# A four-layer hybrid network on one core: the first 400 tokens taken in two parts, with two engines in written order

## The chip, the core and the metric

The kernel runs as one program on one core of a Trainium2 chip. The metric is device time in microseconds (us). Engines are named as in the profile: PE is TensorE (matmuls; PEld are its weight loads), DVE is VectorE, ACT is ScalarE, POOL is GpSimd, SP is SyncE, which here only starts DMA transfers. Each engine works through its own queue in order and waits there for semaphores of the others.

## The reference

`x` (1024 tokens of 1024 features) is put behind 16 learned "meta" tokens, so there are 1040 tokens. Four layers follow, each `h = h + branch(rmsnorm(h))`: attention with a window of 128 tokens, an mLSTM, an HGRN2, and attention again. Only the start of the first attention layer matters here:

```python
def rmsnorm(x, g):
    xf = x.astype(jnp.float32)
    y = xf * lax.rsqrt(jnp.mean(xf * xf, axis=-1, keepdims=True) + EPS)
    return (y * g.astype(jnp.float32)).astype(x.dtype)

def attention_branch(u, w_in, q_gain, k_gain, sinks, w_out, valid, pos):
    q, k, v, z = _split(u @ w_in, (A_W, A_KVW, A_KVW, A_W))
    q = rope(rmsnorm(q.reshape(bsz, lp, A_HEADS, A_HD), q_gain), pos)
    k = rope(rmsnorm(k.reshape(bsz, lp, A_KV, A_HD), k_gain), pos)
    ...
    return (o * jax.nn.silu(z.astype(jnp.float32))).astype(u.dtype) @ w_out
```

`u = rmsnorm(h)` needs, for each token, a sum over all 1024 features before anything can be multiplied with weights.

## The kernel before

**Layout.** Features lie on the 128 partitions in 8 blocks (`KT`, index `k`), tokens along the columns: `x` is a tile of 128 x 8 x 1040. Tokens are worked through in three chunks (`CHUNKS`): columns 0 to 400, 400 to 784, 784 to 1040; below they are chunk 0, 1 and 2.

**Numbers in two halves.** Products run in the type F32R, whose operands are rounded. So each operand is split into a high and a low part (`split`: ACT casts the value to the high part, line 187; DVE subtracts it from the value for the low part, line 188), and a product is three matmuls: high x high, high x low, low x high. The normalised input `u` becomes the tiles `uh` and `ul`; a weight tile becomes `wh` and `wl`, made from a raw tile `wr` in two halves of 512 columns. Raw tiles have 2 buffers (`RAWS`), loaded by SP.

**The norm of a chunk.** For each of the 8 feature blocks ACT squares `x` (`sq`, line 369) and DVE sums the squares (line 373); PE multiplies the sum by a tile of ones in plain f32 to sum over partitions (`stat`, line 381; below: a ones product); ACT makes the reciprocal root by Ln and Exp (lines 353 and 354). `PARTS` is the number of pieces in which this is done per chunk. Then `unit`, for each block: DVE multiplies `x` by gain and reciprocal root (line 407, below: a multiply), and `split` gives `uh` and `ul`. For the 16 meta tokens POOL copies both parts into a small tile `um` (line 412).

**Products.** `proj` makes K and Q (line 254): 8 blocks x 3 matmuls per chunk, with the tokens as the moving side. `proj_v` makes V by blocks of tokens (lines 295 and 299): block 0 is the 16 meta tokens, taken from `um`, blocks 1 to 3 the rest of chunk 0. V's weights come in two tiles (blocks k 0 to 3, and 4 to 7); each token block is so two groups of matmuls, written `vg[0][2 * block + half]`.

**Order.** The PE queue is written out by hand as a list of steps (`steps`); on DVE, ACT and POOL a scheduler places instructions. A step may have a `pre` (a weight load and its split), which is issued up to `LOOKAHEAD` ns ahead. For the first layer the head list is `kv`: two K steps, V's groups of the first half, the other K steps, V's second half. `FIRST` says at which share of the head's cost the norms of chunks 1 and 2 are inserted.

**Names in the change.** `row()` is one of 9 buffers of 128 x 1040; it holds rope tables, K and attention rows. `psa()` and `psj()` take one of 8 PSUM banks. `tc.manual_schedule(engines=...)` makes the named engines keep the order in which the code issues.

Of the kernel before, what the change touches and what calls it, by code (L numbers as in the profile page):

```python
# [9 lines left out]
F32 = mybir.dt.float32  # L10
# [5 lines left out]
P = 128  # L16
# [9 lines left out]
LAST_CHUNKS = [(16, 384), (400, 384), (784, 256)]  # L26
CHUNK_BLOCKS = [(0, 1, 2, 3), (4, 5, 6), (7, 8)]
# [17 lines left out]
PARTS = 2, 2, 2  # L45
FIRST = 0.3, 0.9, 0.3, 0.7
# [62 lines left out]
def hybrid_kernel(ctx: ExitStack, tc: tile.TileContext, ins, out, layers=(0, 1, 2, 3)):  # L109
# [57 lines left out]
    g.memset(um.bitcast(F32), 0.0)  # L167

    def load_x(n):
        c0, cn = CHUNKS[n]  # L170
        for k in range(KT):
            sp.dma_start(x[:, k, c0 : c0 + cn], ins["xT"][k, :, c0 : c0 + cn])

    load_x(0)
    sp.dma_start(ident, ins["ident"])
    sp.dma_start(ngain, ins["ngain"])

# [46 lines left out]
    def weights(src, kind, inrow=False):  # L224
# [5 lines left out]
        for z in (slice(0, 512), slice(512, 1024)):  # L230
            raw = wpool.tile([P, 512], F32, tag="raw", name=nm("wr"), bufs=RAWS)
# [5 lines left out]
    def proj(src, evac, chunks=CHUNKS):  # L237
        st = {}

        def pre():  # L240
            st["w"] = weights(src, "m")

        groups = []
        for n, (c0, cn) in enumerate(chunks):
            grp = []
            for part in range(4):
                def fn(n=n, c0=c0, cn=cn, part=part):
                    if part == 0:
                        st[n] = psj()
                    h, l = st["w"]  # L250
                    acc = st[n]
                    for k in (2 * part, 2 * part + 1):
                        for i, (a, b) in enumerate(((h, uh), (h, ul), (l, uh))):
                            pe.matmul(acc[:, :cn], a[:, k, :], b[:, k, c0 : c0 + cn],  # L254
                                      start=(k == 0 and i == 0), stop=(k == KT - 1 and i == 2))
                    if part == 3:
                        evac(acc, n, c0, cn)

                grp.append([6 * cn * MM, fn, pre if (n == 0 and part == 0) else None])
            groups.append(grp)  # L260
        return groups
# [9 lines left out]
    def proj_v(src0, src1, evac):  # L271
        st = {}

        def pre0():
            st[0] = weights(src0, "v")

        def pre1():
            st[1] = weights(src1, "v")
# [84 lines left out]
    class Norm:  # L363
# [11 lines left out]
        def stat(self, n, part=0, parts=1):  # L375
            cn = CHUNKS[n][1]

            def fn():
                if part == 0:
                    self.ps[n] = psa()  # L380
                pe.matmul(self.ps[n][:, :cn], ones, self.acc[n], start=(part == 0), stop=(part == parts - 1))
                if part == parts - 1:
                    rstd_from(self.ps[n], self.acc[n], cn, D)

            return [4 * cn * MM, fn, None]

        def stats(self, n, parts):

            c0, cn = CHUNKS[n]
# [11 lines left out]
        def unit(self, n, k):  # L401
# [12 lines left out]
            return [0.0, fn, None]  # L414

# [24 lines left out]
    def layer_a(i, j, first, last, fin):  # L440
# [4 lines left out]
        def enter():  # L445
            R["mix"] = mix = new_mix()
            R["masks"] = masks = mix.tile([P, A_MASKS], F32, name=nm("masks"))
            sp.dma_start(masks, ins["a_masks"])
            R["cons"] = cons = mix.tile([P, 34], F32, name=nm("cons"))
            sp.dma_start(cons, ins["a_cols"][j])  # L450
            v.tensor_scalar(cons[:, 0:1], cons[:, 0:1], 0.125, None, op0=ALU.mult)
# [62 lines left out]
        def qk_proj(src, gcol, work, fsplit, ch, scales=None):  # L514
# [45 lines left out]
            return proj(src, evac, ch), [finish(n, *c) for n, c in enumerate(ch)]  # L560
# [152 lines left out]
        kg0, kfin0 = qk_proj(win[0], 1, work_rows(3), k_split(0), CHUNKS)  # L713
        kg1, kfin1 = qk_proj(win[1], 1, work_rows(1), k_split(1), CHUNKS)
        vg = proj_v(win[2], win[3], v_evac)
# [16 lines left out]
        head[0].insert(0, [0.0, enter, None])  # L732
# [596 lines left out]
    steps += norm.stats(0, PARTS[0]) + [norm.unit(0, k) for k in range(KT)]  # L1329
    tail = None  # L1330
    for pos, i in enumerate(layers):
# [10 lines left out]
        if i % 3 == 0:  # L1342
            head, body, oa, ob = layer_a(i, i // 3, tail is None, i == 3, fin)
# [30 lines left out]
    while steps[k][2] is None:  # L1374
        k += 1
    steps[k][2]()
    steps[k][2] = None
    load_x(1)
    k = 0
    for n, (cost, fn, pre) in enumerate(steps):  # L1380
# [5 lines left out]
        if n == 0:  # L1386
            load_x(2)
# [118 lines left out]
```

## Time and profile before

| | |
|---|---|
| median of 3 runs (lowest, highest) | 2607.71 us (2605.75, 2611.24) |
| the profiled execution | 2610.83 us, its span 2609.0 us |
| busy in the span | PE 2558.0 us (98%), DVE 1980.3 (76%), ACT 1725.9 (66%), POOL 154.1 (6%) |
| first product of chunk 0 / of chunk 1 starts | 14.90 us / 36.95 us |
| mean granted PE clock | 0.995 |

Times in rows of the profile are us from the span's start. A row of the timeline gives the start, the length, the engine, the line, the operation, what it writes and reads by the program's names (buffer numbers left out), the shape, a count, and in brackets how long the engine stood idle before it and what ended that. A group row has the count, busy us, the mean in ns, and the idle time before. Neighbouring matmuls overlap in PE's pipeline, so the distance of two starts is what one costs.

### The profile page before, as it was taken

Reading aid. Unit: us, or ns where it says so; the run is one execution under the profiler, and the core shown is the slowest. Engines: PE = TensorE matmul, PEld = TensorE weight load, DVE = VectorE, ACT = ScalarE, POOL = GpSimd, SP = SyncE. Lnnn points to the kernel's source line nnn. Section 1 sums busy time; section 2 is a strip of 40 time slices with the busy share of each in tenths; the row PEclk is TensorE's granted clock in tenths of the full one; section 3 lists DMA queues with packets and bytes.
Section 4 is the critical chain, followed back from the end, with each engine's and each line's share of the span. In section 5 each row is a group of like instructions: output and inputs, shape, how many; then the busy total and the mean of one; then the engine's idle time right before and its main releaser. Section 6 shows DMA issues by size and latency. Waiting matters only on the chain.

```text
span 2609.0 us, 56062 instructions
## 1 busy us (share of the span) xinstructions
PE 2558.0 (98%) x21048; PEld 2459.0 (94%) x21048; DVE 1980.3 (76%) x5487; ACT 1725.9 (66%) x4757; POOL 154.1 (6%) x538
## 2 busy tenths in 40 slices
PE   7999999999999999999999999999999999999999
PEld 6899889899999999999999999999999999999999
DVE  6677777986767676767677788978787978677776
ACT  6777776566464646464646857878585867768872
POOL 1100100000000000000000000201001011000000
PEclk9999999999999999999999999999999999999999
DMA  4111111021111111111110101011110111111112
GB/s 136 56 43 50 46 37 47 17 67 58 41 58 41 58 41 58 41 58 41 55 61 34 57 27 42 30 38 34 34 42 26 42 62 45 54 44 47 53 38 82
DMA packets 74048, 126.81 MB, mean 49 GB/s; under 512 B 11552, under 2 KB 25760, under 8 KB 73776
## 3 DMA queue, kind: packets, MB, share of 16 engines
q1 hardware_dynamic: 73776, 123.23, 14.5%
q8 instruction: 165, 2.70, 0.4%
q14 instruction: 107, 0.88, 0.1%
HBM read 108.34 MB, written 4.26 MB: 43 GB/s over the span
## 4 chain that ended last, share of the span: by engine, by line
PE 81%; DVE 10%; ACT 6%; issue 1%; DMA 1%; POOL 0%; SPq 0%; DVEq 0%; ACTq 0%; POOLq 0%
PE pj L254 39%; PE pj L337 16%; PE pj L299 11%; PE po L682 2%; PE pt L660 1%; PE pm L614 1%; PE pm L615 1%; DVE t L407 1%; PE pa L534 1%; DVE ul L188 1%; PE po L918 1%; PE pj L295 1%; PE pm L890 1%; DVE X L1153 1%; DVE X L1155 1%
## 5 line engine op out<-in xcount | busy, mean ns | idle before, releaser
L254 PE MATMUL pj<-uh,wh 128*128 128x384 f32 (+2 forms) x2592 | 870.9, 336 | 3.7 <-ACT uh L187 3.6
L254 PE MATMUL pj<-ul,wh 128*128 128x384 f32 (+2 forms) x2592 | 835.3, 322 | 2.9 <-DVE ul L188 2.8
L254 PE MATMUL pj<-uh,wl 128*128 128x384 f32 (+2 forms) x2592 | 832.9, 321 | 0.1
L254 PEld LDWEIGHTS pj<-uh,wh 128*128 128x128 f32 x2592 | 491.3, 190 | 24.1 <-issue 12.7
L254 PEld LDWEIGHTS pj<-ul,wh 128*128 128x128 f32 x2592 | 491.2, 190 | 8.7 <-DVE ul L188 5.5
L254 PEld LDWEIGHTS pj<-uh,wl 128*128 128x128 f32 x2592 | 490.9, 189 | 0.5 <-DVE wl L188 0.4
L188 DVE TENSOR_TENSOR wl<-wr,wh 128x512 fp32r<-128x512 f32 x336 | 227.9, 687 | 58.1 <-ACT wh L187 55.4
L340 DVE TENSOR_TENSOR x<-x,pj 128x384 f32<-128x384 f32 (+2 forms) x480 | 235.4, 510 | 43.2 <-PE pj L337 41.3
L187 ACT CAST wh<-wr 128x512 fp32r<-128x512 f32 x337 | 203.3, 616 | 83.0 <-PE pj L337 26.8
L299 PE MATMUL pj<-wh,uh 128*128 128x256 f32 x896 | 258.1, 288 | 0.0
L337 PE MATMUL pj<-yh,wh 128*128 128x384 f32 (+2 forms) x768 | 253.0, 329 | 0.0
L299 PE MATMUL pj<-wh,ul 128*128 128x256 f32 x896 | 252.4, 282 | 0.0
L299 PE MATMUL pj<-wl,uh 128*128 128x256 f32 x896 | 252.3, 282 | 0.0
L337 PE MATMUL pj<-yl,wh 128*128 128x384 f32 (+2 forms) x768 | 247.4, 322 | 3.1 <-DVE yl L188 3.1
L337 PE MATMUL pj<-yh,wl 128*128 128x384 f32 (+2 forms) x768 | 246.8, 321 | 0.0
L299 PEld LDWEIGHTS pj<-wh,uh 128*128 128x128 f32 x896 | 169.3, 189 | 1.1 <-issue 0.3
L187 ACT CAST yh<-r 128x400 fp32r<-128x400 f32 (+2 forms) x144 | 68.6, 477 | 153.2 <-PE pj L337 141.7
L299 PEld LDWEIGHTS pj<-wl,uh 128*128 128x128 f32 x896 | 169.3, 189 | 0.5
L299 PEld LDWEIGHTS pj<-wh,ul 128*128 128x128 f32 x896 | 169.3, 189 | 0.0
L428 ACT ACTIVATE t<-t 128x384 f32<-128x384 f32 (+2 forms) x240 | 117.8, 491 | 76.5 <-DVE t L427 74.8
L427 DVE SCALAR_TENSOR_TENSOR t<-pj,t 128x384 f32<-128x384 f32 (+2 forms) x192 | 98.8, 514 | 78.2 <-ACT t L426 75.3
L337 PEld LDWEIGHTS pj<-yl,wh 128*128 128x128 f32 x768 | 144.9, 189 | 5.0 <-DVE yl L188 4.7
(265 smaller groups left out, 5431.4 us busy)
## 6 DMA issues: line engine op xcount, KB each, us to landing
wr<-in_b_win SPq DMA_DIRECT2D x128, 256.0 KB, 2.6
wr<-in_a_win SPq DMA_DIRECT2D x80, 256.0 KB, 2.7
wr<-in_c_win SPq DMA_DIRECT2D x64, 256.0 KB, 2.7
r<-rowsd SPq DMA_DIRECT2D x16, 520.0 KB, 5.4
wr<-in_a_wout SPq DMA_DIRECT2D x32, 256.0 KB, 2.7
wr<-in_b_wout SPq DMA_DIRECT2D x32, 256.0 KB, 2.6
t<-t SPq DMA_DIRECT2D x96, 48.0 KB, 1.9
wr<-in_c_wout SPq DMA_DIRECT2D x16, 256.0 KB, 2.7
```

What stands on the lines that cost most here:

```text
L187: s.copy(h, src)
L188: v.tensor_tensor(l, src, h.bitcast(F32), op=ALU.subtract)
L254: pe.matmul(acc[:, :cn], a[:, k, :], b[:, k, c0 : c0 + cn], start=(k == 0 and i == 0), stop=(k == KT - 1 and i == 2))
L295: pe.matmul(acc[:48, :256], um[:, k, :], m[:, kk, :], start=(k == 0 and m is wh), stop=(k == KT - 1 and m is wl))
L299: pe.matmul(acc[:cn, :256], a[:, k, c0 : c0 + cn], m[:, kk, :], start=(k == 0 and i == 0), stop=(k == KT - 1 and i == 2))
L337: pe.matmul(acc[:, :cn], a[:, k, mc], b, start=(k == 0 and i == 0), stop=(k == 1 and i == 2))
L340: v.tensor_tensor(x[:, m, c0 : c0 + cn], x[:, m, c0 : c0 + cn], acc[:, :cn], op=ALU.add)
L407: v.scalar_tensor_tensor(u, x[:, k, cs], ngain[:, self.i, k : k + 1], self.acc[n], op0=ALU.mult, op1=ALU.mult)
L427: v.scalar_tensor_tensor(a[:, :cn], z, 0.0, a[:, :cn], op0=ALU.min, op1=ALU.subtract)
L428: s.activation(a[:, :cn], a[:, :cn], AF.Exp)
L534: pe.matmul(st[:, 2 * k : 2 * k + 2], sq[:, z : z + P], R["masks"][:, 0:P:64], start=True, stop=True)
L682: pe.matmul(po[64 * hh : 64 * hh + 64, q0 - c0 : q0 - c0 + nq], V[kb][:kn, vc : vc + 64], ws[hh]["Pt"][:kn, u, ki, :nq], start=(ki == 0), ...
```

## The change

**Two parts.** Chunk 0 is taken as columns 0 to 144 and 144 to 400 (`RANGES[3:]`): each is loaded, squared, summed (in 4 pieces) and split by itself (`first.stats(n, 4)` and the new `halves`), and K's products of chunk 0 are made for each apart, into one PSUM bank. `halves` issues the multiply and the cast of block k ahead of the subtraction of block k - 1, and fills `um` after the last block with one copy on ACT and one on DVE.

**Weights.** K's first weight tile and V's two are loaded into rows (`load_row`), the first two between the loads of the two parts of `x`. Their four (K, V's first) and two (V's second) half splits are put by hand into the two parts' blocks (`take`).

**Order on DVE and ACT.** From `begin` to `end` both keep program order.

**Products of zeros.** `warm(8)` at the start and `warm(4)` ahead of K's first product multiply `um` by ones into banks that nobody reads. `um` is zeroed by DVE in place of POOL. The code issues `warm(4)` after `um` was filled.

**Small moves.** `ident`, and rope's load and scaling, come later on SP's queue; masks and `cons` earlier. `FIRST` puts the norm of chunk 1 later in the head.

```diff
+RANGES = CHUNKS + [(0, 144), (144, 256)]
-PARTS = 2, 2, 2
-FIRST = 0.3, 0.9, 0.3, 0.7
+PARTS = 4, 2, 2
+WARM = 8, 4
+FIRST = 0.45, 0.95, 0.3, 0.7
...
-    load_x(0)
-    sp.dma_start(ident, ins["ident"])
+    load_x(3, 2)
     sp.dma_start(ngain, ins["ngain"])
+    early = [load_row(ins["a_win"][0][k]) for k in (0, 2)]
+    load_x(4, 2)
+    early.append(load_row(ins["a_win"][0][3]))
+
+    def warm(n):
+        def fn():
+            pe.matmul(psa()[:, :384], rones, um.rearrange("p k c -> p (k c)"), start=True, stop=True)
+
+        return [[0.0, fn, None] for _ in range(n)]
...
-            for part in range(4):
+            pieces = halves if (halves and n == 0) else [(c0, cn)]
+            for part in range(4 * len(pieces)):
...
+        def halves(self, n):
+
+            c0, cn = RANGES[n]
+            cs = slice(c0, c0 + cn)
+            u = {}
+
+            def high(k):
+                def fn():
+                    u[k] = tmp()[:, :cn]
+                    v.scalar_tensor_tensor(u[k], x[:, k, cs], ngain[:, self.i, k : k + 1], self.acc[n],
+                                           op0=ALU.mult, op1=ALU.mult)
+                    s.copy(uh[:, k, cs], u[k])
+
+                return [0.0, fn, None]
+
+            def low(k):
+                def fn():
+                    v.tensor_tensor(ul[:, k, cs], u[k], uh[:, k, cs].bitcast(F32), op=ALU.subtract)
+                    if c0 == 0 and k == KT - 1:
+                        s.copy(um[:, :, :NMETA], uh[:, :, :NMETA].bitcast(F32))
+                        v.tensor_copy(um[:, :, 32 : 32 + NMETA], ul[:, :, :NMETA].bitcast(F32))
+
+                return [0.0, fn, None]
+
+            return [high(0)] + [z for k in range(1, KT) for z in (high(k), low(k - 1))] + [low(KT - 1)]
...
-            kv = kg0[0][:2] + vg[0][::2] + kg0[0][2:] + vg[0][1::2]
+            kp, vp = kg0[0], vg[0]
...
+            ordered = tc.manual_schedule(engines={mybir.EngineType.DVE, mybir.EngineType.Activation})
+            begin, end = [0.0, ordered.__enter__, None], [0.0, lambda: ordered.__exit__(None, None, None), None]
+            wk, wv0, wv1 = take(kp[0]), take(vp[0]), take(vp[1])
+            (s0, u0), (s1, u1) = ((first.stats(n, PARTS[0]), first.halves(n)) for n in (3, 4))
+            kv = [begin] + warm(WARM[0]) + s0[:-1] + [wk[0]] + s0[-1:] + u0[:3] + [wk[1]] + u0[3:7] + [wv0[0]]
+            kv += u0[7:11] + [wv0[1]] + u0[11:] + warm(WARM[1]) + kp[:4]
+            kv += [vp[2]] + s1[:4] + [vp[0]] + s1[4:] + u1[:3] + [wv1[0]] + u1[3:7] + [wv1[1]] + u1[7:] + [end]
+            kv += [vp[3], vp[1]] + kp[4:6] + [vp[4], vp[6]] + kp[6:] + [vp[5], vp[7]]
...
-    steps += norm.stats(0, PARTS[0]) + [norm.unit(0, k) for k in range(KT)]
```

What this does to the queues, at two places. The first is ACT from the first casts of `uh` on, before (`wh_98` is K's weight tile, `wh_116` V's first; `t_171` and on are the multiplied blocks; `pa` is the bank of the ones product):

```order
L187 CAST uh<-t_171 128x400
L187 CAST uh<-t_177 128x400
L187 CAST uh<-t_183 128x400
L187 CAST uh<-t_189 128x400
L187 CAST wh_116<-wr_118 128x512
L187 CAST uh<-t_195 128x400
L187 CAST wh_116<-wr_122 128x512
L187 CAST uh<-t_201 128x400
L369 ACTIVATE t_267<-x 128x384
```

and now (`wh_196` is V's first weight tile, from the row `r_96`), from the sixth block of the first part on:

```order
L451 CAST uh<-t_204 128x144
L204 CAST wh_196<-r_96 128x512
L451 CAST uh<-t_210 128x144
L451 CAST uh<-t_214 128x144
L459 CAST um<-uh 128x8x16
L393 ACTIVATE t_267<-x 128x256
L393 ACTIVATE t_269<-x 128x256
L393 ACTIVATE t_274<-x 128x256
L393 ACTIVATE t_276<-x 128x256
L393 ACTIVATE t_289<-x 128x256
```

All squares of the second part stand behind the last cast of the first part and behind `um`. The second place is PE, before, from its first instruction on (`wh_98` and `wl_99` are K's weights):

```order
L381 MATMUL pa_155<-t_144,ones 128x400
L381 MATMUL pa_155<-t_157,ones 128x400
L254 MATMUL pj_232<-uh,wh_98 128x400
L254 MATMUL pj_232<-ul,wh_98 128x400
L254 MATMUL pj_232<-uh,wl_99 128x400
```

and now, from the ones products of the first part on (rows that only repeat are left out; `wh_172` is K's weight tile, `pa_272` the second part's ones product, `wh_310` V's second weight tile):

```order
L405 MATMUL pa_153<-t_161,ones 128x144
L405 MATMUL pa_153<-t_167,ones 128x144
L191 MATMUL pa_221<-um,ones 128x384
...
L278 MATMUL pj_229<-uh,wh_172 128x144
...
L323 MATMUL pj_254<-wh_196,uh 128x256
...
L405 MATMUL pa_272<-t_267,ones 128x256
L405 MATMUL pa_272<-t_274,ones 128x256
L319 MATMUL pj_280<-wh_196,um 48x256
...
L405 MATMUL pa_272<-t_289,ones 128x256
L405 MATMUL pa_272<-t_295,ones 128x256
L323 MATMUL pj_254<-wh_310,uh 128x256
```

The second part's last two ones products stand behind 24 products of K over the first part, 12 of V's block 1 and 8 of `um`, and all of these stand behind a product that reads `um`.

More of the change, by code (lines that the diff above doesn't have):

```diff
@@ L166, in hybrid_kernel, with load_x, load_row @@
     um = cpool.tile([P, KT, 48], F32R, name="um")
[L167 to L172, printed above, removed]
-    load_x(0)
-    sp.dma_start(ident, ins["ident"])
-    sp.dma_start(ngain, ins["ngain"])
+    v.memset(um.bitcast(F32), 0.0)
+    def load_x(n, some):
+        c0, cn = RANGES[n]
+        for k in range(0, KT, some):
+            sp.dma_start(x[:, k : k + some, c0 : c0 + cn],
+                         ins["xT"][k : k + some, :, c0 : c0 + cn].rearrange("k p t -> p k t"))
+    def load_row(src):
+        raw = row()
+        for z in (slice(0, 512), slice(512, 1024)):
+            sp.dma_start(raw[:, z], src[:, z])
+        return raw
+    load_x(3, 2)
+    sp.dma_start(ngain, ins["ngain"])
+    early = [load_row(ins["a_win"][0][k]) for k in (0, 2)]
[5 more added lines that the diff above has]
+        return [[0.0, fn, None] for _ in range(n)]
     layer_pool = [None]
@@ L222, in gate_rows_proj, with weights @@
         return groups
-    def weights(src, kind, inrow=False):
+    late = []
+    def weights(src, kind, inrow=False, row=None):
         if inrow:
@@ L230, in weights @@
         for z in (slice(0, 512), slice(512, 1024)):
+            if row is not None:
+                late.append(lambda z=z: split(row[:, z], h[:, z], l[:, z]))
+                continue
             raw = wpool.tile([P, 512], F32, tag="raw", name=nm("wr"), bufs=RAWS)
@@ L235, in weights, with proj @@
         return h.rearrange("p (k c) -> p k c", k=k), l.rearrange("p (k c) -> p k c", k=k)
-    def proj(src, evac, chunks=CHUNKS):
+    def proj(src, evac, chunks=CHUNKS, row=None, halves=None):
         st = {}
         def pre():
-            st["w"] = weights(src, "m")
+            st["w"] = weights(src, "m", row=row)
         groups = []
@@ L245, in proj, with fn @@
             grp = []
-            for part in range(4):
-                def fn(n=n, c0=c0, cn=cn, part=part):
+            pieces = halves if (halves and n == 0) else [(c0, cn)]
+            for part in range(4 * len(pieces)):
+                def fn(n=n, c0=c0, cn=cn, part=part, pieces=pieces):
                     if part == 0:
@@ L269, in put_v, with proj_v @@
             s.copy(V[:cn, :256], acc[:cn, :256])
-    def proj_v(src0, src1, evac):
+    def proj_v(src0, src1, evac, rows=(None, None)):
         st = {}
         def pre0():
-            st[0] = weights(src0, "v")
+            st[0] = weights(src0, "v", row=rows[0])
         def pre1():
-            st[1] = weights(src1, "v")
+            st[1] = weights(src1, "v", row=rows[1])
         groups = []
@@ L512, in work_rows, with qk_proj @@
             return work
-        def qk_proj(src, gcol, work, fsplit, ch, scales=None):
+        def qk_proj(src, gcol, work, fsplit, ch, scales=None, **how):
             late = {}
@@ L558, in finish @@
                         (D_Q[2], fsplit(lambda: late[n][0], n, c0, cn))]
-            return proj(src, evac, ch), [finish(n, *c) for n, c in enumerate(ch)]
+            return proj(src, evac, ch, **how), [finish(n, *c) for n, c in enumerate(ch)]
         def tile_of(groups, events):
@@ L712, in layer_a @@
                           fin if t == 7 else None, t == 5) for t in (1, 3, 5, 7)}
-        kg0, kfin0 = qk_proj(win[0], 1, work_rows(3), k_split(0), CHUNKS)
+        kg0, kfin0 = qk_proj(win[0], 1, work_rows(3), k_split(0), CHUNKS,
+                            **(dict(row=early[0], halves=RANGES[3:]) if first else {}))
         kg1, kfin1 = qk_proj(win[1], 1, work_rows(1), k_split(1), CHUNKS)
-        vg = proj_v(win[2], win[3], v_evac)
+        vg = proj_v(win[2], win[3], v_evac, early[1:] if first else (None, None))
         qg = {t: qk_proj(win[4 + t], 0, tmps, q_split(t), chunks, t) for t in range(8)}
@@ L731, in layer_a @@
             head.append(tile)
-        head[0].insert(0, [0.0, enter, None])
+        if first:
+            enter()
+        else:
+            head[0].insert(0, [0.0, enter, None])
+        head[0].insert(head[0].index(end) if first else 1, [0.0, rope_load, None])
         body = []
```

40 lines of the change are left out of this document (23 added, 17 removed).

## The prediction

> **What bounds the kernel now.** I read the page's sums first, then busy time by stretch, then the timeline of the first 37 us with its releasers, then means by shape.
>
> ```profile
> span 2609.0 us, 56062 instructions
> 0.00:14.90 14.90, 3.37 (x4) 1.00 (x5) 6.09 (x13) 8.20 (x15) 1.00 (x7) 1.00 0.85 273
> 14.90:36.95 22.05, 20.19 (x117) 17.93 (x118) 16.27 (x33) 13.81 (x29) 11.88 (x20) 0.92 0.56 179
> 36.95:80.00 43.05, 40.15 (x276) 36.93 (x274) 31.65 (x76) 33.77 (x85) 0.92 (x5) 1.00 0.14 42
> 80.00:2609.00 2529.00, 2494.31 (x20656) 2403.12 (x20655) 1926.33 (x5368) 1670.11 (x4630) 140.29 (x506) 1.00 0.14 46
> ```
>
> The columns are the stretch, its length, then busy PE, PEld, DVE, ACT, POOL, the granted clock, DMA share and GB/s. From 80 us on PE is busy 2494.3 of 2529: matmuls bound the kernel, and their number does not change. What can move is when that stream gets going, so I follow one milestone: the first product and the first multiply of the second chunk.
>
> ```profile
> 3.08 1.09 ACT L369 ACTIVATE t<-x 128x400 f32<-128x400 f32 x2 [1.08 <-DMA x<-in_xT]
> 6.51 2.68 ACT L369 ACTIVATE t<-x 128x400 f32<-128x400 f32 x5 [0.80 <-DMA x<-in_xT]
> 10.18 1.70 PE L381 MATMUL pa<-t,ones 128*128 128x400 f32 x2 [0.71 <-DVE t L373]
> 13.66 1.72 DVE L407 SCALAR_TENSOR_TENSOR t<-x,ngain,t 128x400 f32<-128x400 f32 x3
> 14.90 0.70 PE L254 MATMUL pj<-uh,wh 128*128 128x400 f32 x1 [3.02 <-ACT uh L187]
> 16.42 0.54 PE L254 MATMUL pj<-uh,wl 128*128 128x400 f32 x1
> 16.75 0.54 PE L254 MATMUL pj<-uh,wh 128*128 128x400 f32 x1
> 14.99 7.31 POOL um L412 x9
> 23.22 0.41 PE L299 MATMUL pj<-wh,ul 128*128 128x256 f32 x1
> 23.44 0.41 PE L299 MATMUL pj<-wh,uh 128*128 128x256 f32 x1
> 23.57 0.57 DVE L188 TENSOR_TENSOR ul<-t,uh 128x400 fp32r<-128x400 f32 x1
> 26.13 0.28 PE L299 MATMUL pj<-wh,uh 128*128 128x256 f32 x1
> 26.25 0.28 PE L299 MATMUL pj<-wl,uh 128*128 128x256 f32 x1
> 25.98 2.35 DVE L373 TENSOR_TENSOR t<-t,t 128x384 f32<-128x384 f32 x4
> 34.05 1.68 DVE L407 SCALAR_TENSOR_TENSOR t<-x,ngain,t 128x384 f32<-128x384 f32 x3 [0.94 <-ACT t L354]
> 36.95 0.34 PE L254 MATMUL pj<-uh,wh 128*128 128x384 f32 x1
> ```
>
> Rows give start, length, engine and line (the POOL row is one of the chain: nine casts on end, 7.31 us). The 400 columns are squared as x lands, summed by products with ones, multiplied from 13.66; the first real product is at 14.90. All 400 columns stand split into uh and ul at 23.57 + 0.57 = 24.14. Products of 400 columns start 0.33 us apart at first, and those of 256 columns 0.22 at 23.2 but 0.12 at 26.1: PE is at half speed in its first stretch and again at 23, after it waited for POOL's um, and at full speed from 26 on. So chunk 0 costs PE 22.05 us for some 16 us of work (24 products of 400, 88 of 256, two with ones): about 6 us of weakness, beside 14.9 us of start. Multiplies of the second chunk begin at 34.05, its products at 36.95.
>
> **The change, part by part.** Durations for the shapes that the new code uses:
>
> ```profile
> L188 DVE TENSOR_TENSOR wl<-wr,wh 128x512 fp32r<-128x512 f32 x8 | 5.3, 688 | 3.5 <-ACT wh L187 3.3
> L407 DVE SCALAR_TENSOR_TENSOR t<-x,ngain,t 128x400 f32<-128x400 f32 x8 | 4.6, 628 | 0.0
> L188 DVE TENSOR_TENSOR ul<-t,uh 128x400 fp32r<-128x400 f32 x8 | 4.3, 568 | 0.0
> L407 DVE SCALAR_TENSOR_TENSOR t<-x,ngain,t 128x256 f32<-128x256 f32 x8 | 3.7, 478 | 0.6 <-ACT t L354 0.6
> L188 DVE TENSOR_TENSOR ul<-t,uh 128x256 fp32r<-128x256 f32 x8 | 3.3, 418 | 0.1
> L187 ACT CAST wh<-wr 128x512 fp32r<-128x512 f32 x8 | 4.8, 616 | 1.3 <-PE pj L254 0.9 <-DMA wr<-in_a_win 0.3
> L187 ACT CAST uh<-t 128x256 fp32r<-128x256 f32 x8 | 3.2, 407 | 2.1 <-DVE t L407 2.0
> L369 ACT ACTIVATE t<-x 128x256 f32<-128x256 f32 x8 | 2.9, 413 | 0.4 <-DVE ul L188 0.4
> 47.20 0.59 PE L381 MATMUL pa<-t,ones 128*128 128x256 f32 x2
> 49.28 0.47 ACT L353 ACTIVATE t<-pa,eps 128x256 f32<-128x256 f32 x1
> 49.79 0.42 ACT L354 ACTIVATE t<-t 128x256 f32<-128x256 f32 x1
> 23.85 3.24 ACT L369 ACTIVATE t<-x 128x384 f32<-128x384 f32 x7
> ```
>
> No row has 144 columns; a line through 256 and 400 gives, as estimates, 0.36 for a multiply, 0.30 a subtraction, 0.32 a cast or square, 0.37 and 0.32 for Ln and Exp. Three multiplies of 0.628 take 1.72, so DVE overlaps neighbours by 0.08.
>
> *Small parts.* The zeroing of um goes from POOL to DVE, which has nothing to do before the first squares at 3.08: nothing. Masks and cons are asked for earlier, rope later, and neither is waited for before 40.
>
> *Loads.* Squares of piece 1 start at 3.08 and of piece 4 at 6.51: 1.14 us per 200 KB. The first part is four pieces of 144 KB (0.82 us each), last one near 5.3 to 6.0; ngain and the first 256 KB of K weights follow, by 6.8. SP no longer waits for raw weight buffers, since these weights go to row buffers. Masks, cons and weights now stand ahead of x of chunk 1 in the queue, at 0.43 to 0.7 us each; chunk 1 needs x only after 36, so this costs nothing (if it did, one piece is 1.1 us).
>
> *First part (144).* Last squares and sum near 6.2, ones product (four pieces, each after its own sum) to 6.7. The cast of a weight half stands ahead of Ln on ACT (6.8 to 7.4), so Ln and Exp end at 8.1 and multiplies start at 8.2, 5.5 us earlier than now. Then in program order: 8 x (0.36 + 0.30) + 3 x 0.69 = 7.35 of DVE work, less 18 x 0.08 overlap, plus waits. After each pair of multiplies ACT must cast uh (0.32) and a weight half (0.62) before DVE may make wl, and DVE has only one subtraction of 0.30 for that time: three waits of 0.65, and 0.65 at both ends. Sum 8.5: done at 16.7, um at 17.0 (one cast on each engine in place of POOL's 7.31).
>
> *Products of zeros ahead.* Eight from about 1.3 us, off the path. The four later ones read um, which by then is rewritten with the 16 meta columns, so they wait for it, and all of chunk 0's products stand behind them: PE idles from 6.7 to 17.0 though split columns are there from 9 us. Then 4 x 0.33, 24 products of 144 columns, 12 of V, two ones products, 8 of um, two more ones products. At half speed 144 columns are 0.12 by the spacing of 0.33 per 400. No row shows this type with fewer than 256 columns beside a few of 16; the bounds are 0.07 (full speed, one column a cycle) and 0.30 (the rate of the plain-f32 ones product, 1.70 for one of 400 in two passes at half speed, taken to full speed). I take 0.12, since the same line at 400 columns is the nearest row, and keep +4 us as the upper end. 17.0 + 1.3 + 2.9 + 12 x 0.13 + 8 x 0.12 + 4 x 0.45 + 0.2 = 25.7.
>
> TensorE: Matmul & The Clock Gate, in the Trainium skill ("Why this matters for your kernels"), says to warm up with at least 4 us of matmuls; twelve products of zeros are about 4 us, and by that the 24 would run at full speed, 1.4 us less. The row against it here is the idle time of some 10 us in the middle of the twelve, so the sum keeps half speed.
>
> *Second part (256).* Its squares start only behind the first part's casts, near 16.9, and its adds end at 20.3; but its last two ones products stand behind the 44 products above, so Ln waits to 25.7. Ln 0.47, Exp 0.42: multiplies from 26.7. Work 8 x (0.478 + 0.418) + 2 x 0.69 + 0.41 = 8.95, less 1.5 overlap, plus waits of 2.6 (two weight halves of 0.6; evacuations and squares of chunk 1 on ACT 1; the ends 0.4): 36.8. **The 400 columns are split at 36.8, against 24.14.** One statistic of 400 has become two in a row, with PE's products between them.
>
> *Second chunk.* Eight squares of 384 (3.24 for seven) follow on ACT from 36, adds end at 40.3. Its first ones product (39.7) and its second now have 30 products between them (FIRST moved later): 30 x 0.12 + 0.65 + 0.2, and 0.9 for a half-speed stretch in such a thinly fed PE: 45.0. Ln, Exp 1.1: multiplies at 46.2, against 34.05: **+12.2.** Today 9.9 us lie between the last ul and that multiply, then 9.4.
>
> *Behind it* the order is today's on all engines. I add 1 for third-chunk squares that land among K's evacuations (0 if ACT has room, 3.3 if all eight of 0.413 stand in the way), and 1 for a further stretch at half speed (0 to 1.7, half of some 3.4 us as after 14.90): **+14.2.** The waits inside the two parts are the softest terms, 2.6 us each; with half of them the lag is +11.6, and nearly the same again on the other side is +17. With 2.9 us of PE idle in 43.05 (36.95 to 80) little of it can be taken back.
>
> The profiled execution took 2610.83, that is 1.8 above its span and 3.1 above the median of the runs shown (2607.71). From the median: **2622**. A change under 0.2% (5.2 us) cannot be told from none.
>
> **Rivals.**
>
> *Narrow products run at the plain-f32 rate.* For: their width is nowhere in the trace. Against: same type, same line, one column a cycle at 256, 384 and 400. It adds 24 x 0.18 = 4.3 on the path of the second statistic: 2626; with half speed through it 2630.
>
> *The lag is partly taken back.* DVE and ACT wait for PE between chunks today (5.7 us from 28.33 to 34.05); were PE's late order there shorter than I count, and waits up to 80 us gave back the 2.9, +14 becomes +5 to +9: 2613 to 2617. Against: 46.2 is set by PE's own 30 products.
>
> *The change gains (other side).* PE starts warm, and is fed densely: chunk 0's 16 us of full-speed work from 17.0 + 1.3 would end at 34.3, and if PE used the split columns as they come from 9 us, near 30: -3 to -7, 2601 to 2605. It decides if the second part is split by about 25, so that PE never waits for it. For: 6 us of half speed and POOL waits go. Against: PE has only 44 products (5 us) to cover 10 us of DVE work on the second part, which cannot begin before those are done.
>
> **How the numbers follow.** As forecast 0.53 (2617 to 2626); narrow products slow 0.22 (2626 to 2630); partly taken back 0.16 (2608 to 2617); gain 0.09 (2601 to 2607). The range from 2612 to 2630 leaves out the gain and half of the third. Faster by over 0.2%: 0.06, the larger gains; within 0.2%: 0.09, from the third and the smaller gains; slower 0.85.
>
> **What would show it.** Right: first K product near 18, not 9, with the releaser um; PE nearly idle from 26 to 36; multiplies of 256 columns from about 27; last ul of chunk 0 near 37; first multiply of 384 columns at 45 to 48; from 80 us on the same waits as now, 14 us later. The spacing of the 144-column products (0.06 to 0.12, or 0.25 and more) settles the first rival. Wrong: a second statistic before 22, or a first product of 384 columns before 40.

## The result and the profile after

The changed kernel took 2628.58 us (median of 6 runs, 2626.66 to 2631.55), the kernel before 2610.94 in the same comparison (median of 6, 2605.75 to 2612.41): 1.0074 times as long, with a 95% interval of 1.0064 to 1.0083. That is 17.6 us more where 14.2 was forecast. The profiled execution took 2629.03 us with a span of 2627.2 us, 18.2 more than before.

Busy time by stretch of the changed kernel, cut at its own first product of chunk 0 (18.91), first product of chunk 1 (51.99) and about the point that answers to 80 us before; the columns are those of the prediction:

```profile
0.00:18.91 18.91, 6.69 (x20) 5.85 (x21) 9.74 (x30) 10.74 (x31) 0.64 (x6) 1.00 0.90 294
18.91:51.99 33.08, 26.74 (x150) 24.46 (x149) 14.29 (x34) 12.98 (x33) 1.22 (x4) 0.90 0.21 70
51.99:95.93 43.94, 41.27 (x282) 37.75 (x281) 33.28 (x80) 34.41 (x88) 0.89 (x5) 1.00 0.15 45
95.93:2627.20 2531.27, 2493.32 (x20650) 2401.37 (x20648) 1923.88 (x5365) 1668.40 (x4628) 138.86 (x506) 1.00 0.14 46
```

The start of the products costs 4.0 us more than before (18.91 against 14.90), chunk 0 costs 11.0 more (33.08 against 22.05), the next stretch 0.9 (43.94 against 43.05) and all the rest 2.3 (2531.27 against 2529.00). So 15.0 of the 18.2 us are lost before the second chunk's first product. In that stretch DVE is busy for only 14.29 of 33.08 us: it waits.

The timeline of the changed kernel at that place, each row with start, length and, in brackets, what ended the idle time before it:

```profile
8.66 0.65 DVE L449 SCALAR_TENSOR_TENSOR t<-x,ngain,t 128x144 f32<-128x144 f32 x2
17.12 0.23 DVE L460 CAST um<-ul 128x128 fp32r<-128x128 f32 x1
17.50 1.62 PE L191 MATMUL pa<-um,ones 128*128 128x384 f32 x4 [10.74 <-DVE um L460]
18.91 0.33 PE L278 MATMUL pj<-uh,wh 128*128 128x144 f32 x1
23.73 0.41 PE L278 MATMUL pj<-uh,wl 128*128 128x144 f32 x1
23.94 0.51 PE L323 MATMUL pj<-wh,uh 128*128 128x256 f32 x1
26.60 1.56 PE L405 MATMUL pa<-t,ones 128*128 128x256 f32 x4
28.95 1.03 PE L405 MATMUL pa<-t,ones 128*128 128x256 f32 x4
30.02 0.47 ACT L377 ACTIVATE t<-pa,eps 128x256 f32<-128x256 f32 x1 [10.18 <-PE pa L405]
30.97 0.88 DVE L449 SCALAR_TENSOR_TENSOR t<-x,ngain,t 128x256 f32<-128x256 f32 x2 [10.68 <-ACT t L378]
41.05 0.43 DVE L457 TENSOR_TENSOR ul<-t,uh 128x256 fp32r<-128x256 f32 x1
49.84 1.68 DVE L431 SCALAR_TENSOR_TENSOR t<-x,ngain,t 128x384 f32<-128x384 f32 x3 [4.64 <-ACT t L378]
```

The brackets form a chain. PE stands 10.74 us for `um`; then 24 products of K (18.91 to 23.94: 5.03 us, 0.21 each) and 12 of V (23.94 to 26.60: 2.66, 0.22 each) run ahead of the second part's ones products, and 8 of `um` between these; ACT has waited 10.18 us for those, and DVE 10.68 us for ACT. The 400 columns are split at 41.05 + 0.43 = 41.48 (24.14 before), and the second chunk's multiplies start at 49.84 (34.05 before): +15.8.

K's products of 144 columns ran at half speed. This profile's clock column does not show it (1.00 from 18.91 to 23.94); it is read from their spacing, which run 9 below halves. In a second profile of the same kernel (run 10) the column does show it. There the 24 products took the same 5.03 us, at a granted clock of 0.50 (the last column but two):

```profile
19.46:24.49 5.03, 5.03 (x25) 5.03 (x25) 0.85 (x2) 0.74 (x3) 0.00 (x0) 0.50 0.95 321
```

### The profile page after: what moved, and what is told of

It is laid out like the page before. It is cut to its first block, busy times and chain, and to the rows that moved or that the text cites. A ratio compares the mean times of both kernels' runs of the same rounds, so it can differ in the third digit from the quotient of the medians.

```text
span 2627.2 us, 56180 instructions
## 1 busy us (share of the span) xinstructions
PE 2568.0 (98%) x21096; PEld 2469.4 (94%) x21096; DVE 1981.2 (75%) x5507; ACT 1726.5 (66%) x4776; POOL 141.6 (5%) x521
## 4 chain that ended last, share of the span: by engine, by line
PE 78%; DVE 12%; ACT 7%; issue 2%; DMA 1%; SPq 0%; POOL 0%; DVEq 0%; ACTq 0%; POOLq 0%
PE pj L278 37%; PE pj L361 16%; PE pj L323 11%; PE po L735 2%; PE pt L713 1%; PE pm L667 1%; DVE t L431 1%; PE pa L587 1%; PE pm L668 1%; DVE ul L205 1%; ACT Sm L692 1%; PE pj L319 1%; DVE X L1231 1%; DVE X L1229 1%; PE po L994 1%
## 5 line engine op out<-in xcount | busy, mean ns | idle before, releaser
L278 PE MATMUL pj<-uh,wh 128*128 128x384 f32 (+3 forms) x2600 | 873.2, 336 | 1.3 <-ACT uh L204 1.3
L278 PE MATMUL pj<-ul,wh 128*128 128x384 f32 (+3 forms) x2600 | 837.8, 322 | 2.7 <-DVE ul L205 2.6
L278 PE MATMUL pj<-uh,wl 128*128 128x384 f32 (+3 forms) x2600 | 835.3, 321 | 0.1
```

Source lines behind the costliest of these rows:

```text
L278: pe.matmul(acc, a[:, k, :], b[:, k, p0 : p0 + pn], start=(k == 0 and i == 0), stop=(k == KT - 1 and i == 2))
```

## The experiments

Each is followed by one milestone, the first multiply of 384 columns (34.05 before, 49.84 changed), and by its time against the kernel before in the same comparison. The first four were run together.

**1. No zeros that wait for `um`.**

```diff
-WARM = 8, 4
+WARM = 8, 0
```

> The four products of zeros that wait for um are left out (8 stay at the start). Theory A, the second part's statistic is late because PE's queue stands behind um: the first K product starts at 9 to 10 instead of 18.9, K's 24 and V's 12 products are done by about 20, the second part's squares (from 17.0, eight of 0.41, adds to 20.8) then set its ones products, Ln starts at 24 to 26 instead of 30.0, the first multiply of 384 columns at 44 to 46 instead of 49.84, and the run takes 2622 to 2625 against 2628.6 for the changed kernel. Theory B, DVE's and ACT's two statistics in a row set it and PE only follows: Ln stays at 29 to 30 and the run at 2627 to 2630.

Timeline, first product, second part's Ln and the milestone:

```profile
9.06 0.49 PE L278 MATMUL pj<-uh,wh 128*128 128x144 f32 x1 [2.62 <-ACT uh L451]
24.16 0.47 ACT L377 ACTIVATE t<-pa,eps 128x256 f32<-128x256 f32 x1 [4.69 <-PE pa L405]
44.00 1.68 DVE L431 SCALAR_TENSOR_TENSOR t<-x,ngain,t 128x384 f32<-128x384 f32 x3 [4.64 <-ACT t L378]
```

All three are where theory A put them, 5.9 us earlier at Ln and 5.8 at the milestone. The time, 2626.56 us (1.0061, interval 1.0048 to 1.0075), is only 2 us below the changed kernel's, above the 2622 to 2625 of A, and the two intervals overlap. The place in PE's queue does hold the second statistic; how much of it reaches the end is not shown by this run alone.

**2. One part of 400 columns, the rest as changed**, but without zeros in the middle, with `FIRST` as before and with the list of steps fitted to one part.

```diff
-PARTS = 4, 2, 2
-WARM = 8, 4
-FIRST = 0.45, 0.95, 0.3, 0.7
+PARTS = 2, 2, 2
+WARM = 8, 0
+FIRST = 0.3, 0.9, 0.3, 0.7
...
-    load_x(3, 2)
+    load_x(0, 2)
...
-    load_x(4, 2)
...
+            s0, u0 = first.stats(0, PARTS[0]), first.halves(0)
+            kv = [begin] + warm(WARM[0]) + s0[:-1] + [wk[0]] + s0[-1:] + u0[:3] + [wk[1]] + u0[3:5] + [wv0[0]]
+            kv += u0[5:9] + [wv0[1]] + u0[9:11] + [wv1[0]] + u0[11:13] + [wv1[1]] + u0[13:] + [end]
+            kv += kp[:2] + vp[2::2] + vp[:1] + kp[2:] + vp[3::2] + vp[1:2]
```

> The changed kernel without the split: 400 columns in one part (statistic in two pieces, FIRST as before), weights still in rows, DVE and ACT still in program order with the six half splits between the blocks, um still by ACT and DVE, eight zeros at the start, none in the middle. Theory A, two statistics one after another are the cost: the first multiply of 384 columns starts at 35 to 40 (before 34.05, changed 49.84) and the run takes 2609 to 2616. Theory C, the written order of DVE and ACT with the half splits in it is the cost, whatever the parts: that multiply starts after 45 and the run takes 2622 or more.

```profile
DVE wl L204 <- ACT wh L203: 3.0, 5, 0.6
37.95 1.68 DVE L430 SCALAR_TENSOR_TENSOR t<-x,ngain,t 128x384 f32<-128x384 f32 x3 [7.03 <-ACT t L377]
```

The first row is from its waits (total, times, longest): five half splits, for each of which DVE waits 0.6 us for ACT's cast, since the written order leaves it only one subtraction to do meanwhile. The milestone is 3.9 us later than before, the time 2612.84 us (1.0013, 1.0004 to 1.0022). Theory A: of the 17.6 us, what this kernel keeps (weights in rows, the written order, a new order of K's and V's products) accounts for about 3; the rest comes with the split and what the split brought along.

**3. The kernel before, with products of a constant tile alone.**

```diff
+WARM = 30, 26
...
+    def warm(n):
+        def fn():
+            pe.matmul(psa()[:, :P], rones, rones, start=True, stop=True)
+
+        return [[0.0, fn, None] for _ in range(n)]
...
-    steps += norm.stats(0, PARTS[0]) + [norm.unit(0, k) for k in range(KT)]
+    steps += warm(WARM[0]) + norm.stats(0, PARTS[0]) + warm(WARM[1]) + [norm.unit(0, k) for k in range(KT)]
```

> The kernel before, with products of a constant tile alone added (30 of 128 columns ahead of everything, 26 between the last ones product and K's first product; neither reads um). If the half speed of 14.9 to 18.6 and 22 to 25.5 is what chunk 0 loses, and the second chunk's ones product waits for it: K's products of 400 columns stand 0.17 to 0.18 apart from the start, the second chunk's first multiply starts at 31 to 33 instead of 34.05, and the run is 1.5 to 4 us shorter than before. If the split columns are what PE waits for, whatever its clock: 34 and no change within 1 us.

The moving tile is here the tile of ones itself. The products of one stretch (count, their duration, first and last start), then the 26 ahead of K:

```profile
L181 PE MATMUL pa<-ones x29: 414/415/416, 1.2 to 7.2; 128*128 128x128 f32 x29
11.10 6.24 PE L181 MATMUL pa<-ones 128*128 128x128 f32 x26
17.14 0.64 PE L261 MATMUL pj<-uh,wh 128*128 128x400 f32 x1
```

Without a gap for 6 us, the 128-column products stand 6.0 / 28 = 0.214 apart to the end, and so do the later ones, which push K's first product to 17.14. So the run did not make what it was to test: K's products still stand 0.33 apart from there. Milestone 32.86; 2611.55 us (1.0002, 0.9994 to 1.0011).

**4. What one product costs by its width.** The kernel before, with 48 products of each kind put into a busy stage near 1850 us (44.9 us of added work).

```diff
+    zeros = cpool.tile([P, 320], F32R, name="zeros")
+    g.memset(zeros.bitcast(F32), 0.0)
+
+    def widths():
+        for wide, cols in ((320, P), (256, P), (200, P), (144, P), (P, P), (64, P), (144, 64), (64, 64), (64, 32)):
+            acc = psa()
+            for _ in range(48):
+                pe.matmul(acc[:cols, :wide], rones[:, :cols], zeros[:, :wide], start=True, stop=True)
...
+    steps.insert(3000, [0.0, widths, None])
```

> The kernel before, with 48 products each of several widths of a constant tile by columns of the ones tile in a busy stage, outputs not read: 320, 256, 200, 144, 128 and 64 moving columns with 128 weight columns, 144 and 64 moving with 64 weight columns, 64 moving with 32. Theory D, a product cannot be shorter than the load of its weights, and 128 weight columns of this type take as long as 256 moving ones: spacings of 0.14, 0.12, 0.12, 0.12, 0.12, 0.12 us, then 0.06, 0.06 and 0.03. Theory E, a moving side under 256 columns is slow in itself: spacing for 64 weight columns equal to that for 128 weight columns, 0.12 or more. Theory F, one column a cycle at every width: 0.14, 0.12, 0.09, 0.07, 0.06, 0.03 and the changed kernel's 0.213 had another cause.

Each row gives the products of one kind that lie in a stretch, with the first and last start (128\*64 means 64 weight columns):

```profile
L185 PE MATMUL pa<-zeros,ones x46: 308/308/309, 1847.9 to 1854.5; 128*128 128x320 f32 x46
L185 PE MATMUL pa<-zeros,ones x44: 279/281/282, 1854.9 to 1860.0; 128*128 128x256 f32 x44
L185 PE MATMUL pa<-zeros,ones x42: 272/274/281, 1860.7 to 1865.2; 128*128 128x200 f32 x42
L185 PE MATMUL pa<-zeros,ones x42: 272/277/278, 1866.0 to 1870.6; 128*128 128x144 f32 x42
L185 PE MATMUL pa<-zeros,ones x30: 276/277/278, 1876.7 to 1879.9; 128*128 128x64 f32 x30
L185 PE MATMUL pa<-zeros,ones x38: 222/223/224, 1888.3 to 1890.5; 128*64 128x64 f32 x38
L185 PE MATMUL pa<-zeros,ones x43: 192/197/199, 1891.1 to 1892.5; 128*32 128x64 f32 x43
```

Last start less first, divided by the count less one: 0.147 us for 320 columns, 0.119 for 256, then 0.110 for 200, 0.112 for 144, 0.110 for 64; with 64 weight columns 0.059, with 32 it is 0.033. From 200 moving columns down the width no longer matters, the number of weight columns does: theory D. A product of 144 columns has nearly the price of one of 256, 0.11 at full speed and, in the changed kernel, twice that, 0.21, at half. The Trainium skill gives the time of the load (TensorE: Matmul & The Clock Gate, section "LDWEIGHTS (loading the stationary operand)"): it takes the number of weight columns over 1.2 in ns, which is 107, 53 and 27 ns for the three. The spacings of the narrow products agree with it within 6 ns.

**5. `FIRST` as before, all else as changed.** (5 to 8 were run together.)

```diff
-FIRST = 0.45, 0.95, 0.3, 0.7
+FIRST = 0.3, 0.9, 0.3, 0.7
```

> The changed kernel with FIRST as before (0.3, 0.9 in place of 0.45, 0.95), nothing else. Theory A, the second chunk's two ones products were put behind too much of the head by it: in the changed kernel the first of them waits for nothing but its place, so with it the first multiply of 384 columns starts 2 to 4 us earlier than 49.84, at 46 to 48, and the run takes 2624.5 to 2627. Theory B, the place in the list does not matter, since DVE's adds for the second chunk come late anyway: 49 to 50, and 2628 to 2630.

```profile
46.80 2.21 DVE L431 SCALAR_TENSOR_TENSOR t<-x,ngain,t 128x384 f32<-128x384 f32 x4 [3.42 <-ACT t L378]
```

The milestone is 3.0 us earlier, as theory A has it; the time is 2628.07 us (1.0066, 1.0052 to 1.0080), as theory B has it. The two are not reconciled by this run; see 10 and 11.

**6. The second statistic ahead of K's and V's products.**

```diff
-WARM = 8, 4
+WARM = 8, 0
...
-            kv += u0[7:11] + [wv0[1]] + u0[11:] + warm(WARM[1]) + kp[:4]
-            kv += [vp[2]] + s1[:4] + [vp[0]] + s1[4:] + u1[:3] + [wv1[0]] + u1[3:7] + [wv1[1]] + u1[7:] + [end]
+            kv += u0[7:11] + [wv0[1]] + u0[11:] + s1 + kp[:4]
+            kv += [vp[2]] + [vp[0]] + u1[:3] + [wv1[0]] + u1[3:7] + [wv1[1]] + u1[7:] + [end]
```

> The changed kernel with the second part's squares, sums and ones products issued straight behind the first part's halves and ahead of K's and V's products on PE; the four zeros that wait for um left out. Theory A (the second statistic was late only by its place in PE's queue): squares from 17.0, adds to 20.8, Ln at 21 to 23 instead of 30.0, first multiply of 256 columns at 22 to 24 instead of 31, first multiply of 384 at 41 to 43 instead of 49.84, and the run takes 2618 to 2622; earlier than the kernel without the zeros (Ln 24.16, multiply of 384 at 44.0). Theory B (PE's own work is the limit): K's and V's products now start only at 22 to 23, the second chunk's ones products stand behind them, the multiply of 384 stays at 44 or later, and the run takes 2624 or more.

```profile
18.25 3.75 PE L405 MATMUL pa<-t,ones 128*128 128x256 f32 x8 [11.66 <-DVE t L397]
22.04 0.47 ACT L377 ACTIVATE t<-pa,eps 128x256 f32<-128x256 f32 x1 [2.26 <-PE pa L405]
41.69 1.68 DVE L431 SCALAR_TENSOR_TENSOR t<-x,ngain,t 128x384 f32<-128x384 f32 x3 [5.41 <-ACT t L378]
```

Ln 8.0 us earlier than in the changed kernel, the milestone 8.2: the second statistic was late by its place in PE's queue, as theory A says. 5.9 of the 8.0 us come without the four zeros alone (run 1), so the order of the products is worth some 2. The time is 2624.29 us (1.0052, 1.0039 to 1.0066), 2 us more than A allowed and within what theory B gave.

**7. As 6, with `FIRST` as before.** The edits of 5 and 6 together.

> As the kernel before this one (second statistic ahead of the products, no zeros in the middle), and FIRST as before too, so that of the change stay the split, the weights in rows and the written order. Theory A, what stays costs the part that is DVE's and ACT's own (two statistics in a row, half splits between): the multiply of 384 starts at 39 to 42, between the kernel with one part (37.95) and the changed kernel (49.84), and the run takes 2613 to 2619, slower than one part (2612.8). Theory B, the split pays once nothing stands in its way: the multiply of 384 before 36 and the run under 2609.

The milestone is 39.77, the time 2622.28 us (1.0044, 1.0032 to 1.0057): within theory A at the first, 3 us above it at the second, and far from B. It lies apart from one part (1.0004 to 1.0022), so the split in this form is a loss also without the zeros in the middle and with its statistic ahead on PE.

**8. Wide zeros on the kernel before.**

```diff
+WARM = 22, 16
...
+    zeros = cpool.tile([P, 320], F32R, name="zeros")
+    v.memset(zeros.bitcast(F32), 0.0)
+
+    def warm(n):
+        def fn():
+            pe.matmul(psa()[:, :320], rones, zeros, start=True, stop=True)
```

(with the list of steps as in 3)

> The kernel before, with products of a constant tile of zeros, 320 columns wide: 22 ahead of everything and 16 between the last ones product and K's first product. Theory A, the 128-column products of the earlier run kept PE at half speed (0.213 apart to 20.6) since they fill it to half; wide ones bring it to full speed: first full-speed stretch from 5 to 9, K's products of 400 columns 0.18 apart from the first, at 15 to 15.6, the multiply of 384 at 31 to 32.5, the run 2606 to 2609. Theory B, the width of the zeros does not matter to the clock: half speed to about 20 again, the multiply of 384 at 33 or later, and 2610 to 2612.

```profile
L184 PE MATMUL pa<-zeros,ones x9: 468/468/468, 1.8 to 3.9; 128*128 128x320 f32 x9
L184 PE MATMUL pa<-zeros,ones x11: 307/308/310, 4.4 to 5.9; 128*128 128x320 f32 x11
10.56 2.82 PE L184 MATMUL pa<-zeros,ones 128*128 128x320 f32 x16
33.29 1.68 DVE L417 SCALAR_TENSOR_TENSOR t<-x,ngain,t 128x384 f32<-128x384 f32 x3 [0.94 <-ACT t L364]
```

0.26 apart to 3.9, 0.15 from 4.4: the wide products reach full speed, as theory A says of the clock, and K's products of 400 columns stand 0.18 apart at 15.4. The milestone and the time are theory B's, 33.29 and 2611.41 us (1.0002, 0.9993 to 1.0011). So the speed of K's first products is not what sets the second chunk's start in the kernel before. The run did not free all of chunk 0 of half speed, though: V's products behind them stood 0.21 apart again, at a granted clock of 0.53:

```profile
22.00:25.00 3.00, 3.00 (x16) 3.00 (x16) 2.90 (x8) 3.00 (x8) 2.45 (x6) 0.53 1.02 314
```

In the second profile of the kernel before (run 11) V's products stand 0.12 apart at a clock of 1.00 (23 to 26 us; 0.59 in the first profile), and the milestone is 32.40 instead of 34.05. So half speed on V's products goes with about 1.7 us at the milestone, by these two profiles.

**9. The changed kernel, with PE kept busy while it waits for `um`.** (9 to 11 were run together.)

```diff
-WARM = 8, 4
+WARM = 8, 1
...
+    def hot(n):
+        def fn():
+            pe.matmul(psa()[:, :320], rones, zeros, start=True, stop=True)
...
-            kv += u0[7:11] + [wv0[1]] + u0[11:] + warm(WARM[1]) + kp[:4]
+            kv += u0[7:11] + [wv0[1]] + u0[11:] + hot(56) + warm(WARM[1]) + kp[:4]
```

> The changed kernel with one product that reads um in place of four, and 56 products of a constant tile of zeros, 320 columns wide, ahead of it (0.147 us each at full speed: 8.2 us, from 6.7 to about 15). PE still waits for um at 17, but no longer idles for ten microseconds. Theory A, the step that was sized too small (from um to the second part's Ln, 8.7 forecast, 12.5 measured) is half speed on products that 128 weight columns hold to 0.11: K's 24 products stand 0.11 apart instead of 0.213, V's 12 0.12 instead of 0.213, Ln starts at 25 to 26.5 instead of 30.0, the multiply of 384 at 45 to 46.5 instead of 49.84, the run takes 2624 to 2626.5. Theory B, products of 144 columns take 0.21 whatever the clock: K's spacing and Ln (29 to 30) stay, and the run takes 2627 to 2630.

```profile
6.11 8.48 PE L194 MATMUL pa<-zeros,ones 128*128 128x320 f32 x56
16.70 0.41 PE L200 MATMUL pa<-um,ones 128*128 128x384 f32 x1 [2.11 <-DVE um L469]
16.95 0.23 PE L287 MATMUL pj<-uh,wh 128*128 128x144 f32 x1
19.47 0.27 PE L287 MATMUL pj<-uh,wl 128*128 128x144 f32 x1
19.58 0.33 PE L332 MATMUL pj<-wh,uh 128*128 128x256 f32 x1
21.05 1.02 PE L414 MATMUL pa<-t,ones 128*128 128x256 f32 x4
23.94 0.47 ACT L386 ACTIVATE t<-pa,eps 128x256 f32<-128x256 f32 x1 [4.89 <-PE pa L414]
43.73 1.68 DVE L440 SCALAR_TENSOR_TENSOR t<-x,ngain,t 128x384 f32<-128x384 f32 x3 [4.63 <-ACT t L387]
```

PE waits for `um` as ever, but with a gap of 2.1 us instead of 10.7. K's 24 products take 19.58 - 16.95 = 2.63 us (0.11 each) where they took 5.03, V's 12 take 1.47 where they took 2.66, three zeros fewer 1.2 less. From the product that reads `um` to Ln it is 7.2 us instead of 12.5. Theory A; Ln and the milestone (43.73) are even earlier than it said, as multiplies began 0.8 earlier in this run (7.85). The granted clock is 1.00 over K's products. The time is 2624.63 us (1.0049, 1.0037 to 1.0062).

**10 and 11. The changed kernel and the kernel before, once more, unchanged.**

> The changed kernel once more, unchanged, for a second profile. Theory A, the lag at the second chunk is fixed by the order and what is added behind 80 us falls by chance with the half-speed stretches: the multiply of 384 at 48.5 to 51 again, half-speed stretches behind 80 us at other places, the span's end anywhere from +14 to +20 on the kernel before. Theory B, the later part is as fixed as the first: the same stretches at the same places, +18 within 0.5.

> The kernel before once more, unchanged, as the control for the same: the multiply of 384 columns at 33.5 to 35.5, and if the half-speed stretches behind 80 us fall by chance, its steps from 130 us on stand up to 3 us off those of the first profile, either way; if they are fixed, within 0.5.

The changed kernel took 2630.74 us (1.0076, 1.0061 to 1.0092), with the milestone at 51.21 and a span of 2629.6, 2.4 longer than its first and 20.6 above the first of the kernel before. Both lie just outside theory A (48.5 to 51, +14 to +20). The kernel before took 2615.73 us in the one run, with the milestone at 32.40 and a span of 2614.0: ahead of its first profile by 1.65 us at 34 and behind it by 5.0 at the end, both more than was expected. The rows of 75 to 130 us of the kernel before, first profile and second (the clock is the last column but two):

```profile
75.00:130.00 55.00, 49.91 (x367) 44.75 (x367) 39.96 (x121) 40.21 (x136) 6.33 (x19) 0.97 0.20 59
```

```profile
75.00:130.00 55.00, 50.34 (x339) 45.47 (x340) 36.53 (x111) 37.90 (x128) 5.71 (x18) 0.88 0.20 59
```

In the same 55 us the second execution got 28 matmuls less done, at a mean clock of 0.88 instead of 0.97. So one kernel's executions differ by some us in the half-speed stretches behind 75 us (theory A in kind, larger in size), and a single profile's lag there is no effect of an edit. The milestone itself differs by 1.4 and 1.65 us between the two profiles of one kernel, so a smaller step in it says little. That limits what can be read off 1, 5, 6 and 7: their milestones are earlier by 3 to 10 us, their times by 0.5 to 6. In the profiles of 7 and 12 the clock from 75 to 130 is 0.88 as well, in both of the changed kernel 0.97, in that of 9 it is 1.00. Whether the edits bring such stretches on, or a handful of executions happened to have them, stays open.

**12. The split with each cost so far taken away.** The edits of 7, and

```diff
-            kv += u0[7:11] + [wv0[1]] + u0[11:] + s1 + kp[:4]
+            kv += u0[7:11] + [wv0[1]] + u0[11:] + hot(72) + s1 + kp[:4]
```

> The split with each of the costs found so far taken away: second statistic ahead of K's and V's products, FIRST as before, no product that waits for um, and 72 products of a constant tile of zeros, 320 columns wide, between the two parts' ones products, so that PE is at full speed when K's products begin. Theory A, what is left is DVE's and ACT's own (two statistics in a row, six half splits between the blocks), which no clock of PE shortens: the multiply of 384 columns at 37 to 39.5, against 39.77 without the zeros, 37.95 with one part and 32.4 to 34.05 in the two profiles of the kernel before, and the run takes 2613 to 2620. Theory B, half speed was all that kept the split from paying: the multiply of 384 before 34 and the run at 2609 or less, which would be a version better than both kernels.

```profile
22.05 1.75 ACT L402 ACTIVATE t<-x 128x384 f32<-128x384 f32 x4
24.81 0.87 DVE L458 SCALAR_TENSOR_TENSOR t<-x,ngain,t 128x256 f32<-128x256 f32 x2
DVE wl L214 <- ACT wh L213: 4.9, 5, 2.4
40.36 2.21 DVE L440 SCALAR_TENSOR_TENSOR t<-x,ngain,t 128x384 f32<-128x384 f32 x4 [4.39 <-ACT t L387]
```

2617.52 us (1.0030, 1.0018 to 1.0042), in theory A's range; the milestone at 40.36 is 0.9 later than A said. With `FIRST` as before, four squares of the second chunk fall into the written order ahead of the second part's multiplies, which could have started near 22; but in run 7 they stand there too (multiplies from 25.78). What differs from run 7 is PE behind the split: from the second chunk's first ones product to its second it takes 7.4 us (30.94 to 38.35) at a clock of 0.57 from 31 to 35, where run 7 takes 5.8 (31.92 to 37.76) at 1.00.

Nothing beats the kernel before. Against it in each comparison, the changed kernel loses 17.6 us; without the four zeros 16.6 (run 1); with the second statistic ahead as well 14.0 (run 6); with `FIRST` as before 12.0 (run 7); with PE kept busy 7.9 (run 12); and with one part in place of two 2.9 (run 2). The intervals of the last two overlap (1.0018 to 1.0042 and 1.0004 to 1.0022), so what the split by itself still costs in time is not shown. The products of a constant tile on the kernel before change nothing that can be measured.

## What the prediction had right, and the step that failed

The direction and the mechanism held. The step that failed is a term of the sum: the price of K's and V's products between `um` and the second part's Ln, 2.9 + 1.56 = 4.5 us forecast, 5.03 + 2.66 = 7.7 measured, which is 3.2 of the 4.3 us by which Ln came late.

**Right: the direction and the mechanism.** First K product at 18.91 with `um` as the releaser in front (forecast near 18); second part's multiplies at 30.97 with PE's ones products as the cause of the wait; the 400 columns in two statistics one after the other; PE nearly idle from 30 to 35 (busy 1.25 of 5 us) where 26 to 36 was forecast. Run 6 shows the step that the sum rests on: with the second statistic ahead of the products on PE, and without the zeros that wait for `um`, the second Ln comes 8.0 us earlier. Run 1 shows that the wait for `um` is 5.9 of it.

The time lies near the upper end of the range of 2612 to 2630, above the likeliest case's own 2617 to 2626. That the range reached so far is in part luck: its upper end was kept for narrow products at the plain-f32 rate, which is not what happened. Three of the signs that were named came out elsewhere: the last `ul` of chunk 0 ended at 41.48 and not near 37, the first multiply of 384 columns started at 49.84 and not at 45 to 48, and the spacing of the 144-column products, 0.21, lies in neither of the two ranges between which it was to decide.

**The step that failed: the products between `um` and the second part's Ln.** The sum had 17.0 + 1.3 + 2.9 + 1.56 + 0.96 + 1.8 + 0.2 = 25.7; Ln came at 30.02. Term by term: `um` 0.5 late (17.50 against 17.0); the four zeros 1.41 against 1.3; K's 24 products 5.03 against 24 x 0.12 = 2.9; V's 12 products 2.66 against 12 x 0.13 = 1.56; ones products and `um`'s eight 3.42 against 2.96. Two mistakes are in the two big ones. The price of a 144-column product was scaled down from 400 columns, but its weights take nearly as long to load as 256 columns take to stream (0.110 and 0.119 us in run 4). And V's products were put at full speed although K's, right ahead of them, were put at half. Run 9 takes the half speed away and gets the forecast's length for the same stretch: 2.63 for K, 1.47 for V. The upper bound that the text kept, 0.30 each, was on the right side; it was given to a rival about plain f32, which is not the mechanism: at full speed 144 columns cost 0.11 and not 0.30. The rule on warming up that was weighed there (the Trainium skill, TensorE: Matmul & The Clock Gate) would have made the sum smaller still; with the ten idle microseconds in the middle the products ran at half speed, as the text held against it, and without them, in run 9, at full speed.

**From there on.** Second part 10.5 us (30.97 to 41.48) against 10.1; from the last subtraction to the second chunk's multiply 8.4 against 9.4. The forecast had 0.9 in it for a half-speed stretch, which did not come here (PE's clock 1.00 from 43.56 to 47.82); in the second profile of the changed kernel it did (0.71 from 43.38 to 49.20), and the same way took 9.9. 25.7 became 30.0 (+4.3), +0.4, -1.0: together, within rounding, the +15.8 where +12.2 stood. The two allowances of 1 us behind it came to 2.4 in the profiles (+18.2 at the end), but by runs 10 and 11 that figure is inside what two executions of one kernel differ by.

**Rivals.** Narrow products at the plain-f32 rate: wrong mechanism, though the time fell where it said (2626 to 2630), because the load of the weights brings the price from 0.12 to 0.21 in its place. Lag partly taken back: no, the span's lag grew. Gain: its condition was a split second part by about 25; it came at 41.5, and even in run 12, with the second Ln at 21.23 and multiplies from 24.81, the part was split only at 33.66. What stands against it is what the prediction named there, the work of DVE on the second part.

## What to carry to other kernels

Before a tile is split, ask what now stands between its two halves on every in-order queue: here a statistic of the second half went behind the products of the first on PE, and ACT and DVE stood for ten microseconds, most of it because those products themselves waited for `um`. A narrower moving side saves nothing once its time is shorter than the load of its weights (for 128 weight columns of this type the limit lies between 200 and 256 columns, by run 4), so splitting columns multiplies the products without making them cheaper. Work that only keeps an engine warm must not read anything that arrives late.

## What was not expected of the hardware

Products of a constant tile do not bring PE to full speed merely by being without a gap. In run 3 the 128-column ones stayed 0.214 apart through 6 us, while in run 8 the 320-column ones went from 0.26 to 0.15 apart near 4. (The two also differ in what moves, ones in run 3 and zeros in run 8. For the width speak K's 24 products of 144 columns in run 10, which move real numbers and stayed 0.21 apart for 5 us without a gap, at a clock of 0.50; no run changes the width alone.) In run 4 PE had been at full speed for all sets down to 64 columns, and fell to half within that one, still without a gap:

```profile
1876.60:1880.20 3.60, 3.60 (x35) 3.60 (x34) 1.00 0.02 5
1880.30:1887.00 6.70, 6.70 (x49) 6.70 (x49) 0.52 0.00 0
```

(busy PE, busy PEld, then the clock: 3.60 of 3.60 us busy at 1.00, 6.70 of 6.70 at 0.52.) What these have in common is that PE streams for half of the time or less and loads weights for the rest; that this is what the clock goes by is an inference, not shown (the 128-column set of run 4, 5 us long, kept full speed). The Trainium skill (TensorE: Matmul & The Clock Gate, Part 1, "What you observe") has back-to-back products of 128 columns in bf16 go to full speed after some 4 us; here, with operands of four bytes, they did not, and for this type the measurement decides.
